# A decoder step on one core: the first part of the time mixing, with its row mixing on ScalarE and one convolution piece to a pair

## The chip, the core and the metric

The kernel runs on one core of a Trainium2 chip, and all of it is one launch. Its engines each work through their own queue in order: TensorE (PE in the profile; its weight loads are PEld), VectorE (DVE), ScalarE (ACT), GpSimd (POOL), and SyncE (SP), which issues most of the DMAs. The metric is the device time of one execution in microseconds (us); lower is better.

## The reference, cut to what matters

One layer of a decoder is computed for 256 prompt rows and 8 samples of 4 rows, 288 rows in all, with a model width of 2048. The part that the change touches is this (`p` holds the weights; the prompt and each sample have their own previous row):

```
p_rkv, p_conv = proj[..., :3 * G_RWKV], proj[..., 3 * G_RWKV:]
p_rkv_prev = jnp.concatenate([(h_last @ w_in[:, :3 * G_RWKV])[:, None], p_rkv[:, :-1]], axis=1)
rkv = p_rkv + (p_rkv_prev - p_rkv) * p['mu_rkv'][l].reshape(-1)
...
kk = (k * p['k_k'][l]).reshape(B, T, N_HEADS, HEAD_SIZE)
kk = kk / jnp.maximum(jnp.sqrt(jnp.sum(kk * kk, axis=-1, keepdims=True)), 1e-12)
k = k * (1 + (a - 1) * p['k_a'][l])
y, S = wkv7_scan(st_wkv[l].astype(f32), r_h, w_h, k_h, v_h, kk, kk * a_h)
...
bg, cg, hc = jnp.split(p_conv, 3, axis=-1)
zc, conv_buf = causal_dwconv(st_conv[l], cg * hc, p['conv_w'][l])
o_conv = bg * zc
```

After it come the output projection and a gated feed-forward block, which the change leaves alone.

## The kernel before

The program has five stages: the conditioning vectors and the first norm; the projection to r, k and v with the first low-rank products; the first part of the time mixing; its second part; the output projection with the feed-forward block. The change lies in the third.

All activations stand transposed, 128 features by 288 rows. The table `A` holds r, k and v as 24 tiles (3 kinds by 8 pairs of heads). Matrix products in float32 are done as three products of a high and a low part: `split` makes the two parts of 1024 weight columns with a cast on ScalarE (L154) and a subtraction on VectorE (L156), and `mm3` issues the three matmuls (L164 to L166).

The third stage starts with `lora2`: 48 matmuls, and 16 sigmoids on ScalarE (L590). Then a loop runs over the 8 pairs. For each pair `lerp` mixes r, k and v with the rows one step earlier (`before`, L341 and L342, and L576); `first` normalises k, scans the decay and scales the operands (a chain over ScalarE, VectorE, TensorE and at its end GpSimd, L597 to L625); `blocks_of` multiplies the pair's 64-row blocks on TensorE and writes them to DRAM. Between these stand `step(cv)` and `step(rest)`. The first emits one piece of the convolution's projection: one weight tile of 1 MB, two splits, 48 matmuls of 288 columns; there are 24 pieces, and after every second one `conv_evac` takes the result out of PSUM. The second emits one step of a conditioning vector (a 1 MB load and 4 matmuls of 512 columns).

After the loop `substitute` reads the blocks back and inverts them by substitution: a sequence of small products and additions on VectorE and GpSimd (L664, L665, 3 steps and then 31), a copy (L666), and three DMAs to DRAM. `drain(cv)` emits the pieces that are left. The second part of the time mixing (`second`, L774 on) begins with loads of the inverse from DRAM (L994 to L998).

The order in the queues of the engines is fixed when the kernel is built: a list scheduler of the framework takes the instructions by their place in the program and by when it thinks they are ready. The scratch tiles of the stage lie by hand in one buffer, `ws`; a ring hands them out in turn, and a tile is written again only when its readers are done.

Of the kernel before, what the change touches and what calls it, by code (L numbers as in the profile page):

```python
# [10 lines left out]
F32 = mybir.dt.float32  # L11
F32R = mybir.dt.float32r
AF = mybir.ActivationFunctionType
# [3 lines left out]
P = 128  # L17
# [6 lines left out]
NP = G // P  # L24
T0 = 256
NB = 8
TS = 4
NT = T0 + NB * TS
NL = T0 + NB * (TS + 1)
LW = NL + 2  # L30
# [49 lines left out]
def kernel(ctx, tc, i, o):  # L80
# [101 lines left out]
    shO = cst.tile([P, 9, KT], F32, name="shO")  # L182
    coO = cst.tile([P, 18, NP], F32, name="coO")
    omka = cst.tile([P, NP], F32, name="omka")

    actx = ctx.enter_context(ExitStack())
    Ap = actx.enter_context(pool("Ap"))
# [52 lines left out]
    cwv = vec[:, 272:296]  # L240
# [74 lines left out]
    def step(g):  # L315
        if g is rest:
            done[0] += 1
        next(g, None)
# [20 lines left out]
    def before(d, a, eng=V):  # L339

        eng.tensor_tensor(d, a[:, 1:1 + NT], a[:, 2:2 + NT], SUB)  # L341
        eng.tensor_tensor(s4(d[:, T0:])[:, :, 0], a[:, 2 + NT:LW], s4(a[:, 2 + T0:2 + NT])[:, :, 0], SUB)  # L342

    def s4(ap):
        return ap.rearrange("p (b t) -> p b t", t=4)
# [9 lines left out]
    with actx:  # L355
# [3 lines left out]
        with pool("x1") as xp:  # L359
# [83 lines left out]
            for bi, (k0, nk) in enumerate(blocks):  # L443
                hs = hn
                last = bi == len(blocks) - 1
                width, part = 2048 // nk, 1024 // nk
                npc = 3 * G // width
                for nb in range(npc):
                    raw = load_piece(w_in, k0, nk, nb * width, width)
                    for ct in range(width // P):  # L450
                        cw = ct * P % part
                        if cw == 0:
                            hv, lv = split(raw[:, :, ct * P:ct * P + part], nk)
                        cw = slice(cw, cw + P)
                        acc = accbank()
                        for kk in range(nk):
                            mm3(acc[:, :NL], hv[:, kk, cw], lv[:, kk, cw],
                                actH[:, k0 + kk], actL[:, k0 + kk], kk == 0, kk == nk - 1)
                        t = nb * width // P + ct
                        if bi == 0:  # L460
                            S.copy(A[:, t, 2:LW], acc[:, :NL])
                        else:
                            V.tensor_tensor(A[:, t, 2:LW], acc[:, :NL], A[:, t, 2:LW], ADD)  # L463
                    if bi == 0 and nb == 0:
                        nc.sync.dma_start(con[:, first:], i['consts'][:, first:NCONST - 2 * P])
                        raw = rawtile()[:, :2 * P]
                        nc.sync.dma_start(raw, i['consts'][:, NCONST - 2 * P:])
                        S.copy(conr, raw.rearrange("p (n x) -> p n x", x=P))
                        turn_rows(2, 4)
                        V.tensor_scalar(omka, kav, -1.0, 1.0, MUL, ADD)  # L470
                        setup.close()
                    for _ in range(0 if last else plan[bi][nb]):
                        step(ada)
                        count += 1
                        if count == 2 * (k0 + nk - blocks[0][1] + blocks[bi + 1][1]):
                            hn = make_h(*blocks[bi + 1])
                    if last and nb == 2:
                        with tc.issue_after(cur['ld'].ins):
                            nc.sync.dma_start(dX, xT)
                    if nb == 0:  # L480
                        raw = rawtile()
                        rw = raw[:, :nk * 448].rearrange("p (k n) -> p k n", k=nk)
                        for name, a, w in (('decay_lora1', 0, 96), ('iclr_lora1', 96, 96), ('gate_lora1', 192, 256)):
                            nc.sync.dma_start(rw[:, :, a:a + w], i[name][0][k0 * P:(k0 + nk) * P]
                                              .rearrange("(k p) n -> p k n", p=P))
                        lps = [bank() for _ in range(4)]
                        for kk in range(nk):
                            if kk % 2 == 0:
                                lwv = split(rw[:, kk:kk + min(2, nk)], min(2, nk))
                            lora1_k(k0 + kk, kk, nk, hs[kk], lwv, lps)  # L490
                        for cidx in range(4):
                            w = 96 if cidx < 2 else 128
                            if bi == 0:
                                S.copy(L1[:w, cidx], lps[cidx][:w, :NT])
                            else:
                                V.tensor_tensor(L1[:w, cidx], lps[cidx][:w, :NT], L1[:w, cidx], ADD)
# [42 lines left out]
        def views(off, *shapes):  # L539
            out = []  # L540
            for shape in shapes:
                ap, off = view(off, shape)
                out.append(ap)
            return out, off

        def ring(off, shape, n):
            aps, off = views(off, *[shape] * n)
            count = [0]

            def turn():  # L550
                count[0] += 1
                return aps[count[0] % n]
            return turn, off

        if True:
            ldr, off = ring(0, (NT,), 2)
            er, off = ring(off, (NT,), 8)
            ntr, off = ring(off, (4, CL), 2)
            nsr, off = ring(off, (NB, TS), 2)
            nrr, off = ring(off, (TS,), 2)  # L560
            cgr, off = ring(off, (2, NT), 1)
            zr, off = ring(off, (NC,), 2)
            zbr, off = ring(off, (NC,), 1)
            (ocv, UL, ULs, TL, TTL, TTs), off = views(off, (NP, NT), (32, 32), (TS, TS), (32, 32), (32, 32), (TS, TS))
            st, off = ring(off, (256,), 1)
            stg, off = ring(off, (256,), 1)

# [3 lines left out]
            def lerp(n, p):  # L571

                t = n * NP + p
                d = ldr()
                before(d, A[:, t])
                V.scalar_tensor_tensor(A[:, t, 2:2 + NT], d, murkv[:, t:t + 1], A[:, t, 2:2 + NT], MUL, ADD)  # L576

            def lora2():
                raw = rawtile().rearrange("p (n x) -> p n x", n=2)
# [12 lines left out]
            def first(p):  # L592
# [23 lines left out]
                V.scalar_tensor_tensor(kk, k, kkv[:, p:p + 1], rn, MUL, MUL)  # L616
                V.scalar_tensor_tensor(XA[:, p], kk, -1.0, cx, MUL, MUL)
                V.tensor_tensor(kk, kk, a, MUL)
                V.tensor_scalar(a, a, kav[:, p:p + 1], omka[:, p:p + 1], MUL, ADD)
                V.tensor_tensor(k, k, a, MUL)  # L620
                GP.tensor_tensor(XB[:, p], kk, ipv, MUL)
                GP.tensor_tensor(k, k, ipv, MUL)
# [71 lines left out]
            def conv_evac(part, j, acc, cg, z):  # L694
                if part == 0:
                    S.copy(cg, acc[:, :NT])
                elif part == 1:
# [5 lines left out]
                    V.tensor_tensor(s6(zb[:, 258:NC])[:, :, 2:6], s4(acc[:, T0:NT]), s4(cg[:, T0:]), MUL)  # L703
                    GP.tensor_copy(coO[:, 0:2, j], zb[:, 256:258])
                    GP.tensor_copy(coO[:, 2:18, j].rearrange("p (b t) -> p b t", t=2), s6(zb[:, 258:NC])[:, :, 4:6])
                    V.tensor_scalar(z[:, :NC - 2], zb[:, 0:NC - 2], cwv[:, j:j + 1], None, MUL)
                    for t in (1, 2):
                        V.scalar_tensor_tensor(z[:, :NC - 2], zb[:, t:NC - 2 + t], cwv[:, 8 * t + j:8 * t + j + 1],
                                               z[:, :NC - 2], MUL, ADD)
# [7 lines left out]
            for p in range(NP):  # L717
                for n in range(3):
                    lerp(n, p)
                first(p)  # L720
                if p:
                    blocks_of(p - 1)
                step(cv)
                step(cv)
                for _ in range(2):
                    step(rest)
# [553 lines left out]
```

## Time and profile before

| | us |
|---|---|
| median of 3 runs | 1698.98 |
| the runs | 1698.98, 1683.72, 1699.15 |
| the profiled execution | 1694.01 |
| its span | 1692.2 |
| PE busy | 1630.8 (96%) |
| DVE busy | 1160.7 (69%) |
| ACT busy | 713.6 (42%) |
| POOL busy | 387.1 (23%) |

The span is that of the profiled execution's instructions, and the busy times are sums over it. The shares are means over five stages, and so they don't say what bounds one of them; the stage of the change runs from about 268 to 491 us of the span. Matmuls overlap, so a stretch in which PE is fully busy can still run at either of two clocks; the granted clock (PEclk, 1.00 is full speed) tells them apart.

### The profile page before, as it was taken

To read this page: it belongs to the slowest core of one execution; us is meant where nothing else is said; L and a number is where in the kernel's file an instruction comes from. 1 tells how busy PE (TensorE), PEld (TensorE's weight loads), DVE (VectorE), ACT (ScalarE), POOL (GpSimd) and SP (SyncE) were. 2 spreads that over 40 slices of the span, in tenths; PEclk is the share of its full clock that TensorE was granted. 3 is DMA by queue.
4 is the path that set the end of the run, shared out by engine and by line. 5 is a ranking of instruction groups with operands and counts; after the bars stand their busy time and mean duration, and the time that the engine had idled before them with its cause. 6 is when DMAs were issued, how large, how long until landed. Compare 5 with 4: busy or idle time off the path is not lost.

```text
span 1692.2 us, 32395 instructions
## 1 busy us (share of the span) xinstructions
PE 1630.8 (96%) x12713; PEld 1481.5 (88%) x12713; DVE 1160.7 (69%) x2464; ACT 713.6 (42%) x1281; POOL 387.1 (23%) x853
## 2 busy tenths in 40 slices
PE   6999999999889999899899999999999999999996
PEld 3778898889866666699799999999999999999996
DVE  3687798977846665554776676757676766757586
ACT  4543355444234433333654343443434343434444
POOL 2132011221633232100143031221213131221212
PEclk9999999999979999999999999999999999999998
DMA  8897865688567667954654545545545445445532
GB/s 274 287 334 270 281 214 191 198 254 258 160 181 248 215 232 247 331 175 141 224 175 150 175 157 168 174 152 173 163 162 174 151 150 183 166 156 169 174 125 76
DMA packets 238306, 333.61 MB, mean 197 GB/s; under 512 B 35698, under 2 KB 180826, under 8 KB 229546
## 3 DMA queue, kind: packets, MB, share of 16 engines
q1 hardware_dynamic: 234937, 324.55, 58.8%
q0 software_dynamic: 2848, 6.20, 1.1%
q8 instruction: 100, 1.64, 0.4%
q10 hardware_dynamic: 368, 0.79, 0.2%
q14 instruction: 53, 0.43, 0.1%
HBM read 321.63 MB, written 9.89 MB: 196 GB/s over the span
## 4 chain that ended last, share of the span: by engine, by line
PE 84%; DVE 8%; ACT 3%; DMA 2%; POOL 1%; issue 1%; SPq 0%; DVEq 0%; ACTq 0%
PE acc L164 22%; PE acc L166 22%; PE acc L165 22%; PE ada L298 5%; DVE wlo L156 2%; PE acc L298 2%; ACT whi L154 1%; PE wb L298 1%; PE wa L298 1%; PE acc L301 1%; PE wa L301 1%; PE ada L301 1%; DMA A<-in_x_sample_dram 1%; PE wb L164 1%; PE wb L166 0%
## 5 line engine op out<-in xcount | busy, mean ns | idle before, releaser
L164 PE MATMUL acc<-actH,whi 128*128 128x288 f32 (+1 forms) x2368 | 707.1, 299 | 9.0 <-ACT whi L154 5.2
L165 PE MATMUL acc<-actL,whi 128*128 128x288 f32 (+1 forms) x2368 | 703.6, 297 | 0.1
L166 PE MATMUL acc<-actH,wlo 128*128 128x288 f32 (+1 forms) x2368 | 700.9, 297 | 2.8 <-DVE wlo L156 2.7
L156 DVE TENSOR_TENSOR wlo<-raw,whi 128x1024 fp32r<-128x1024 f32 (+1 forms) x391 | 478.6, 1226 | 217.3 <-ACT whi L154 211.0
L154 ACT CAST whi<-raw 128x1024 fp32r<-128x1024 f32 x400 | 417.6, 1048 | 475.9 <-PE acc L165 409.3
L164 PEld LDWEIGHTS acc<-actH,whi 128*128 128x128 f32 x2368 | 448.6, 189 | 20.2 <-ACT whi L154 9.7
L166 PEld LDWEIGHTS acc<-actH,wlo 128*128 128x128 f32 x2368 | 447.8, 190 | 5.6 <-DVE wlo L156 4.6
L165 PEld LDWEIGHTS acc<-actL,whi 128*128 128x128 f32 x2368 | 448.3, 189 | 0.4 <-DVE actL L161 0.3
L164 PE MATMUL acc<-gH,whi 128*128 128x288 f32 x704 | 209.1, 297 | 1.7 <-DVE rd L1051 1.7
L166 PE MATMUL acc<-gH,wlo 128*128 128x288 f32 x704 | 210.4, 299 | 0.0
L165 PE MATMUL acc<-gL,whi 128*128 128x288 f32 x704 | 205.7, 292 | 0.0
L1144 POOL COPY uO<-ub 128x2 f32<-128x2 f32 x88 | 24.6, 280 | 548.6 <-ACT ub L1142 548.6
L164 PEld LDWEIGHTS acc<-gH,whi 128*128 128x128 f32 x704 | 132.3, 188 | 3.8 <-PE acc L166 3.7
L165 PEld LDWEIGHTS acc<-gL,whi 128*128 128x128 f32 x704 | 134.0, 190 | 0.0
L166 PEld LDWEIGHTS acc<-gH,wlo 128*128 128x128 f32 x704 | 132.0, 187 | 0.7
L1049 DVE SCALAR_TENSOR_TENSOR xT<-acc,modT,xT 128x256 f32<-128x256 f32 x192 | 91.7, 477 | 27.6 <-PE acc L166 27.6
L301 PE MATMUL ada<-raw,cT 128*32 128x512 f32 x576 | 109.3, 623 | 0.0
L298 PE MATMUL ada<-raw,cT 128*32 128x512 f32 x192 | 100.0, 623 | 1.0 <-DMA raw<-in_ada_w_dram 0.7
L1149 DVE SCALAR_TENSOR_TENSOR uz<-ub,cw,uz 128x304 f32<-128x304 f32 x176 | 96.5, 548 | 4.3
L1141 POOL COPY ub<-sF 128x16 f32<-128x16 f32 x88 | 71.2, 809 | 103.9 <-ACT sF L1045 103.9
L1147 DVE TENSOR_SCALAR uz<-ub,cw 128x304 f32<-128x304 f32 x88 | 33.1, 376 | 49.5 <-ACT ub L1143 49.5
L463 DVE TENSOR_TENSOR A<-acc,A 128x296 f32<-128x296 f32 x96 | 44.2, 463 | 29.0 <-PE acc L166 28.5
(449 smaller groups left out, 1985.0 us busy)
## 6 DMA issues: line engine op xcount, KB each, us to landing
raw<-in_ada_w_dram SPq DMA_DIRECT2D x88, 1024.0 KB, 5.2
raw<-in_ffn_up_dram SPq DMA_DIRECT2D x88, 1024.0 KB, 5.1
raw<-in_w_in_dram SPq DMA_DIRECT2D x48, 1024.0 KB, 7.4
raw<-in_ffn_down_dram SPq DMA_DIRECT2D x44, 1024.0 KB, 5.2
raw<-in_w_out_dram SPq DMA_DIRECT2D x16, 1024.0 KB, 5.9
raw<-in_ada_w_dram SPq DMA_DIRECT2D x16, 512.0 KB, 8.0
dX<-xT SPq DMA_DIRECT2D x1, 2304.0 KB, 16.0
xT<-dX POOLq DMA_DIRECT2D x4, 576.0 KB, 9.3
```

Source lines behind the costliest of these rows:

```text
L154: S.copy(hi, raw)
L156: (GP if cur['share'] and cur['turns'] % cur['share'] == 0 else V).tensor_tensor(lo, raw, hi.bitcast(F32), SUB)
L164: E.matmul(acc, wh, xh, start=start, stop=False)
L165: E.matmul(acc, wh, xl, start=False, stop=False)
L166: E.matmul(acc, wl, xh, start=False, stop=stop)
L298: ins = calls[0]().ins
L301: c()
L463: V.tensor_tensor(A[:, t, 2:LW], acc[:, :NL], A[:, t, 2:LW], ADD)
L1049: V.scalar_tensor_tensor(xT[:, t, :T0], acc[:, :T0], modT[:, m, t, 0:1], xT[:, t, :T0], MUL, ADD)
L1141: GP.tensor_copy(bv[:, :, 0:2], sF[:, :, j].rearrange("p (b t) -> p b t", t=2))
L1147: V.tensor_scalar(z[:, :NC - 2], b[:, 0:NC - 2], cw[:, 0, j:j + 1], None, MUL)
L1149: V.scalar_tensor_tensor(z[:, :NC - 2], b[:, t:NC - 2 + t], cw[:, t, j:j + 1], z[:, :NC - 2], MUL, ADD)
```

## The change

The row mixing is written in another way. Before, VectorE took the difference of the earlier and the present row and added it, weighted, to the present row (three instructions, all on VectorE). Now ScalarE scales the earlier rows by mu (two instructions, the second for the 8 first rows of the samples) and the present rows by 1 - mu (`omur`, made once), and VectorE adds the two. The step that turns `a` into 1 + (a - 1) k_a and the first tap of the convolution move from VectorE to ScalarE. The rings of `first` and of `lerp` have twice as many tiles; the new ones share room with tiles of `substitute`. The loop emits one convolution piece to a pair and not two, so that 16 of 24 pieces stand behind the loop, and not 8.

```diff
+    omur = cst.tile([P, 24], F32, name="omur")
...
+                        V.tensor_scalar(omur, murkv, -1.0, 1.0, MUL, ADD)
...
-            ldr, off = ring(0, (NT,), 2)
-            er, off = ring(off, (NT,), 8)
+            ld_, off = views(0, *[(NT,)] * 2)
+            e_, off = views(off, *[(NT,)] * 8)
...
-            (ocv, UL, ULs, TL, TTL, TTs), off = views(off, (NP, NT), (32, 32), (TS, TS), (32, 32), (32, 32), (TS, TS))
+            more, _ = views(off + NP * NT, *[(NT,)] * 10)
+            (ocv, UL, TL, TTL, ULs, TTs), off = views(off, (NP, NT), (32, 32), (32, 32), (32, 32), (TS, TS), (TS, TS))
+            ldr, er = turns(ld_ + more[8:]), turns(e_ + more[:8])
...
             def lerp(n, p):
                 t = n * NP + p
-                d = ldr()
-                before(d, A[:, t])
-                V.scalar_tensor_tensor(A[:, t, 2:2 + NT], d, murkv[:, t:t + 1], A[:, t, 2:2 + NT], MUL, ADD)
+                a, d, mu = A[:, t], ldr(), murkv[:, t:t + 1]
+                S.activation(d, a[:, 1:1 + NT], AF.Copy, scale=mu)
+                S.activation(s4(d[:, T0:])[:, :, 0], a[:, 2 + NT:LW], AF.Copy, scale=mu)
+                S.activation(a[:, 2:2 + NT], a[:, 2:2 + NT], AF.Copy, scale=omur[:, t:t + 1])
+                V.tensor_tensor(a[:, 2:2 + NT], a[:, 2:2 + NT], d, ADD)
...
-                V.tensor_scalar(a, a, kav[:, p:p + 1], omka[:, p:p + 1], MUL, ADD)
+                S.activation(a, a, AF.Identity, scale=kav[:, p:p + 1], bias=omka[:, p:p + 1])
...
-                    V.tensor_scalar(z[:, :NC - 2], zb[:, 0:NC - 2], cwv[:, j:j + 1], None, MUL)
+                    S.activation(z[:, :NC - 2], zb[:, 0:NC - 2], AF.Copy, scale=cwv[:, j:j + 1])
...
                 step(cv)
-                step(cv)
                 for _ in range(2):
                     step(rest)
```

The change also moves instructions in the queues. Three places matter. (Line numbers of the changed kernel are up to 10 higher: L154 and L160 stay, L590 is now L600, the table load L726, the three instructions of the row mixing on ScalarE L583 to L585, the last one on VectorE L586, and L664 and L665 are now L674 and L675.)

ScalarE at the start of the stage, before: the casts of the last projection, the two casts of `lora2`, the first cast of the convolution, and then the sigmoids.

```order
L154 CAST whi<-raw 128x1024 x5
L160 CAST whi<-raw 96x1024 x2
L154 CAST whi<-raw 128x1024
L590 ACTIVATE XA<-wb,vec 128x288
L590 ACTIVATE XA<-wa,vec 128x288
```

The same place in the changed kernel:

```order
L154 CAST whi<-raw 128x1024 x5
L160 CAST whi<-raw 96x1024 x2
L583 ACTIVATE ws<-A,vec 128x288 x2
L600 ACTIVATE XA<-wb,vec 128x288
L600 ACTIVATE XA<-wa,vec 128x288
```

And what follows there behind the sixteenth sigmoid, down to the convolution's first two casts:

```order
L726 ACT_TABLE_LOAD
L584 ACTIVATE ws<-A,vec 128x8
L585 ACTIVATE A<-A,omur 128x288
L584 ACTIVATE ws<-A,vec 128x8
L585 ACTIVATE A<-A,omur 128x288
L583 ACTIVATE ws<-A,vec 128x288
L623 ACTIVATE ws<-ws 128x288
L584 ACTIVATE ws<-A,vec 128x8
L585 ACTIVATE A<-A,omur 128x288
L607 ACTIVATE ws<-A,vec 128x288
L624 ACTIVATE ws<-ws 128x288
L625 ACTIVATE ws<-ws 128x288
```

The first cast for the convolution has gone from ahead of the sigmoids to behind all of these.

VectorE where the loop ends and the substitution starts, before: behind the last reduction of the blocks (L640) three more splits stand ahead of the substitution's first product (L664).

```order
L640 TENSOR_REDUCE ws<-ws 32x4
L794 COPY ws<-A 128x288
L801 TENSOR_TENSOR ws<-A,pend 128x32
L156 TENSOR_TENSOR wlo<-raw,whi 128x1024 x2
L711 TENSOR_TENSOR ws<-acc,ws 128x256
L712 TENSOR_TENSOR ws<-acc,ws 128x32
L711 TENSOR_TENSOR ws<-acc,ws 128x256
L712 TENSOR_TENSOR ws<-acc,ws 128x32
L156 TENSOR_TENSOR wlo<-raw,whi 128x1024
L664 TENSOR_TENSOR ws<-ws 128x3
```

The same place in the changed kernel (L650 is the reduction, L265 adds a bias to a conditioning vector that TensorE has transposed):

```order
L650 TENSOR_REDUCE ws<-ws 32x4 x2
L810 TENSOR_TENSOR ws<-A,pend 128x32
L810 TENSOR_TENSOR ws<-XB,pend 128x32
L803 COPY ws<-A 128x288
L265 TENSOR_TENSOR modT<-ada,vec 128x4x9 x4
L674 TENSOR_TENSOR ws<-ws 128x3
L156 TENSOR_TENSOR wlo<-raw,whi 128x1024
L675 TENSOR_TENSOR ws<-ws 128x3
L156 TENSOR_TENSOR wlo<-raw,whi 128x1024
```

No split is left between the last reduction and the first product.

VectorE further on, in the changed kernel, from the first of the 31 larger steps: eight of them stand in one row (L674 with up to 192 columns, each followed by its L675) before the next split.

```order
L674 TENSOR_TENSOR ws<-ws 128x156
L675 TENSOR_TENSOR ws<-ws 128x6x26
L674 TENSOR_TENSOR ws<-ws 128x175
L675 TENSOR_TENSOR ws<-ws 128x7x25
L674 TENSOR_TENSOR ws<-ws 128x192
L675 TENSOR_TENSOR ws<-ws 128x8x24
L156 TENSOR_TENSOR wlo<-raw,whi 128x1024
L674 TENSOR_TENSOR ws<-ws 128x184
```

The kernel before has the same eight in a row; what differs is the number of splits ahead of them. Behind the substitution's last step VectorE has 21 further splits of the convolution in the changed kernel, and none in the kernel before.

## Rows read from the trace of the kernel before

**Rows 1.** Stretches: start:end, us, busy us of five engines (instructions), PEclk, DMA share, GB/s.

```profile
268.00:284.00 16.00, 13.98 (x98) 11.12 (x97) 15.77 (x37) 14.36 (x28) 2.65 (x9) 1.00 0.51 161
311.00:413.00 102.00, 102.00 (x808) 89.08 (x804) 82.39 (x177) 44.10 (x77) 23.47 (x47) 1.00 0.80 256
456.00:460.00 4.00, 0.20 (x2) 0.15 (x1) 3.83 (x13) 0.50 (x1) 2.56 (x8) 0.91 0.21 33
460.00:466.00 6.00, 6.00 (x25) 6.00 (x26) 5.35 (x19) 1.91 (x3) 1.14 (x6) 0.50 0.38 153
484.00:502.00 18.00, 15.22 (x136) 11.47 (x134) 5.26 (x15) 3.97 (x13) 4.14 (x17) 0.50 0.78 212
```

**Rows 2.** Timeline of PE: start, us, instruction, and in brackets idle time with its releaser.

```profile
295.39 0.68 PE L635 MATMUL wb<-XA,XB 64*64 64x64 f32 x8 [1.36 <-POOL XB L621]
...
430.06 0.29 PE L164 MATMUL acc<-actH,whi 128*128 128x288 f32 x1
...
440.00 0.30 PE L164 MATMUL acc<-actH,whi 128*128 128x288 f32 x1
...
459.88 0.58 PE L164 MATMUL acc<-actH,whi 128*128 128x288 f32 x1 [3.80 <-DVE ws L703]
...
487.17 0.60 PE L301 MATMUL acc<-T,ws 32*32 32x32 f32 x8 [2.73 <-DMA T<-dT]
```

**Rows 3.** Groups by line and shape, 311 to 413 us: count | busy, mean ns | idle before.

```profile
L156 DVE TENSOR_TENSOR wlo<-raw,whi 128x1024 fp32r<-128x1024 f32 x24 | 29.6, 1246 | 14.0 <-ACT whi L154 13.9
...
L576 DVE SCALAR_TENSOR_TENSOR A<-ws,vec,A 128x288 f32<-128x288 f32 x9 | 5.6, 625 | 0.1
L621 POOL TENSOR_TENSOR XB<-ws 128x288 f32<-128x288 f32 x6 | 5.3, 882 | 6.0 <-DVE A L620 5.6 <-DVE ws L342 0.4
L619 DVE TENSOR_SCALAR XB<-XB,vec,omka 128x288 f32<-128x288 f32 x6 | 3.8, 632 | 0.0
L341 DVE TENSOR_TENSOR ws<-A 128x288 f32<-128x288 f32 x8 | 3.6, 450 | 0.0
...
L342 DVE TENSOR_TENSOR ws<-A 128x8 f32<-128x8 f32 x9 | 2.6, 290 | 0.0
L597 ACT ACTIVATE ws<-A,vec 128x288 f32<-128x288 f32 x4 | 2.1, 536 | 9.9 <-POOL A L622 9.9
L706 DVE TENSOR_SCALAR ws<-ws,vec 128x304 f32<-128x304 f32 x4 | 1.5, 372 | 0.0
```

**Rows 4.** Timeline of ACT at the start of the stage.

```profile
269.18 1.05 ACT L154 CAST whi<-raw 128x1024 fp32r<-128x1024 f32 x1
...
276.92 0.61 ACT L590 ACTIVATE XB<-wa,vec 128x288 f32<-128x288 f32 x1
277.55 1.28 ACT L716 ACT_TABLE_LOAD   x1
...
280.29 1.03 ACT L154 CAST whi<-raw 128x1024 fp32r<-128x1024 f32 x1
```

**Rows 5.** Timeline of DVE behind the loop.

```profile
433.99 0.35 DVE L664 TENSOR_TENSOR ws<-ws 128x31 f32<-128x31 f32 x1
...
441.12 0.52 DVE L665 TENSOR_TENSOR ws<-ws 128x192 f32<-128x192 f32 x1
...
474.75 0.42 DVE L711 TENSOR_TENSOR ws<-acc,ws 128x256 f32<-128x256 f32 x1
```

**Rows 6.** The chain of waits from 413 us: start, us, engine, tile and line.

```profile
413.56 0.60 PE wb L635 x8
...
474.36 2.06 ACT ws L666
...
490.94 0.62 PE wa L892 x2
...
522.29 0.36 PE wa L892 x2
...
547.33 0.36 PE wa L892 x2
```

More of the change, by code (lines that the diff above doesn't have):

```diff
@@ L547, in ring, with turns @@
             aps, off = views(off, *[shape] * n)
+            return turns(aps), off
+        def turns(aps):
             count = [0]
@@ L551, in turn @@
                 count[0] += 1
-                return aps[count[0] % n]
-            return turn, off
+                return aps[count[0] % len(aps)]
+            return turn
         if True:
-            ldr, off = ring(0, (NT,), 2)
-            er, off = ring(off, (NT,), 8)
+            ld_, off = views(0, *[(NT,)] * 2)
+            e_, off = views(off, *[(NT,)] * 8)
             ntr, off = ring(off, (4, CL), 2)
```

## The prediction

> **What bounds the kernel now.** I read the stretches first, then the timelines of TensorE, ScalarE and VectorE in the stage of the change, then the chain of waits. From 311 to 413 us, six turns of the pair loop, TensorE is busy all the time at the full clock, and its timeline has no idle time there; VectorE is busy 82.4 us of 102 and ScalarE 44.1 [rows 1]. So a turn takes 17.0 us and TensorE sets it. Before that VectorE is the bound: from 268 to 284 us it is busy 15.8 us of 16 [rows 1], and at 295.39 TensorE still waits for the pair's operands [rows 2]. Behind the loop the substitution and the splits share VectorE. Its 31 larger steps begin at 433.99 [rows 5] and end with the copy at 474.36 [rows 6], just as the last pieces of the convolution are taken out of PSUM at 474.75 [rows 5]. On the way TensorE waits 3.80 us at 459.88 for a PSUM bank whose reader stands behind substitution steps [rows 2], and after that gap its clock is 0.50, the lower of its levels (1.2 and 2.4 GHz), for 6 us [rows 1]. Then the second part waits for the inverse to come back from DRAM (2.73 us at 487.17, [rows 2]), and the clock is 0.50 again from 484 to 502 us [rows 1]. The first pair of that part takes 31.4 us (490.94 to 522.29), the second 25.0 (to 547.33) [rows 6].
>
> The edits relieve VectorE in a loop that TensorE bounds. They can win only at the start, in the substitution and at the hand-over; TensorE's own work is the same.
>
> **The prices.** A matmul costs 0.1325 us: 75 of them lie between the two of its rows [rows 2], so a piece (48) costs 6.4 us. A row mixing cost VectorE 0.45 + 0.29 + 0.63 = 1.37 us [rows 3]. Now VectorE keeps one addition, 0.45, and ScalarE gets two activations with a scale from a table, nearest to L597 at 0.54, and a small one. No row prices the small one: at least nothing, at most 0.54; I take 0.3, near VectorE's 0.29 for the same 8 columns. The step with k_a goes from 0.63 on VectorE to 0.54 on ScalarE, the first tap from 0.37 to 0.54 [rows 3].
>
> Per pair, VectorE had 82.4 / 6 = 13.7 us, with 9 of 18 mixings in that stretch (the L576 in [rows 3]; the others ran earlier). It loses two splits (2.5, [rows 3]), 1.5 mixings (2.1), 0.6 for k_a and, by my estimate, 0.8 of the convolution's evacuation, and gains three additions (1.4): 9.1. ScalarE had 44.1 / 6 = 7.4. It loses two casts (2.1, [rows 4]) and half the evacuation copies (0.2), and gains three mixings (4.1), k_a (0.5) and taps (0.2): 9.9. TensorE loses one piece: 17.0 - 6.4 = 10.6. TensorE remains the bound, but ScalarE comes within 0.7 us of it and VectorE within 1.5.
>
> **Term A, the start: +5.** The convolution's first cast went ahead of the sigmoids at 269.18 [rows 4]; now it is queued behind them, the table load and eleven activations. The sigmoids and the load end at 278.8 as before (277.55 + 1.28). The eleven, three of them small, follow each other every 0.1 to 0.45 us, together 3.7: the cast starts at 282.5, its split ends at 284.7 (1.03 + 1.25). Until the first blocks TensorE then has 54 matmuls (7.2), a conditioning step (0.9) and the second pair's group sum (0.7): the blocks start at 293.5 and not at 295.4. But by then the kernel before had done 97 convolution matmuls: 43 fewer are 5.7 us, two conditioning steps more give 1.8 back. 5.7 - 1.8 - 1.9 = 2 us behind. TensorE also stands nearly idle from 277 to 282.5, longer than the gap of 3.80; half clock for 6 us costs 3. Ends 0 and 8: the waiting loop work may fill the gap, or the clock may stay low for longer.
>
> **Term B, the pairs: +6.** At 10.6 us a pair the path from one group sum to that pair's blocks gets tight: in queue order all of a turn's VectorE work but one split lies on it (9.1 - 1.2 = 7.9 us), then the product on GpSimd (0.88, [rows 3]) and about 1 us of hand-overs, 9.8 in all. It is hidden while nothing else stands in that path. In the fourth to fifth pair an evacuation with 2.7 us of VectorE work stands there, and in the last three the chains of pairs 6 and 7 run interleaved, with two group sums ahead of one split: 3 + 3. Ends 0 and 19 (second rival). The DMAs of a pair, 3 MB in 10.6 us, are 290 GB/s against 256 at a DMA share of 0.80 [rows 1]; the loads are issued a turn ahead, so I price them at nothing; without that cover they too fall under the upper end.
>
> **Term C, behind the loop: +8.** Before, from the last blocks (413.56, [rows 6]) to 474.75 it took 61.2 us for 384 matmuls, the blocks and a transpose, 53 of work: 8 lost. Now no split stands between the last blocks and the substitution, and VectorE first waits for a transpose that TensorE does only behind piece 7: TensorE waits 2 us for the next split. The eight larger steps in a row take 7.6 us (433.99 to 441.64, [rows 5]), with the small steps and the split behind them 10; TensorE has 5 us of matmuls left then: 5 lost. The evacuation behind substitution steps recurs twice, 4 and 3, and 2 are lost at bank changes: 16. Then 21 splits' worth of matmuls run undisturbed. 16 - 8 = 8; ends 0 (as before) and 14 (half clock after each gap). SP's queue has one convolution load ahead of the reads of the blocks and fifteen behind; the splits wait for VectorE at that point anyway.
>
> **Term D, the hand-over: -5.** From 474.75 to the first product with the inverse, 490.94, it is 16.2 us. Now the inverse is in DRAM some 70 us earlier, and its loads wait only for SP's queue and for room that the last splits free; then the 2.73 and the copy's 2.06 [rows 2, 6] are gone. Ends -7 and 0. **Term E: -5.** Without that wait the clock can stay up: the first pair's 31.4 against 25.0 gives at most 6.3. Ends -6.3 and +3.
>
> Twice the ring costs nothing in time; its readers are done before the last blocks, so the substitution's reads don't wait for it. `omur` is one instruction of 24 columns.
>
> The sum: 5 + 6 + 8 - 5 - 5 = +9 on the profiled execution's 1694.0: **1703 us**. The median of the runs, 1699.0, lies 5 above that execution, the fastest run 10 below; I leave the sum as it is and allow for it in the range.
>
> **The rivals.** First, **faster**: the substitution, early and under 16 pieces, costs TensorE nothing, because the splits keep ahead of it. For it: before, the same steps cost TensorE no more than 8 us. Against it: the queue order just shown. Then the 8 lost before go too: -8 - 5 - 5 = -18, with A and B at nothing: 1676. Chance 0.17, partly taken.
>
> Second, **slower**: ScalarE becomes the bound of the loop. Place: k_a on ScalarE, queued behind the next pair's mixing and a cast, and the product on VectorE and then on GpSimd that wait for it before the blocks can start. It decides when that path exceeds 10.6 us; with a ScalarE of 9.9 busy and two waits of 1.5 us for VectorE, a pair takes 13: 8 x 2.4 = 19 in place of 6, in all 1716, with half clock after such gaps 1722. For it: 9.9 against 10.6. Against it: the ring lets the mixing run a pair ahead. Chance 0.21. The Trainium skill, "ScalarE: Activation LUTs", Rules for kernel authors, would have additions and multiplications on VectorE and not on ScalarE. The rows agree as to sums: a mixing rises from 1.37 us on one engine to 0.45 + 1.38 on two; by the rule alone, with nothing overlapping, 24 mixings cost 24 x 0.46 = 11 us.
>
> Third, **no change**: what moves lies under TensorE's constant work, and A to E cancel within 5 us: 1694 to 1699. Chance 0.12. My forecast has 0.50.
>
> The range, 1683 to 1723, takes in these cases but the outer ends, and the 5 us between execution and median. 1% is 17 us, about what can be told from no change here; by the cases, faster by more has 0.12, slower by more 0.21.
>
> **What the profile would show.** A: no convolution matmul between 277 and 282 us, low clock behind it. B: turns of 10.6 to 12 us; at 13 or more, with waits for XB, the second rival. C: a gap of some 5 us about 20 us behind the last blocks, then solid matmuls for 65 us. D: under 12 us from the last convolution matmul to the first product with the inverse. E: a first pair of some 26 us. Wrong would be: VectorE fully busy in the loop, or no gap in the substitution.

## The result, and the profile after

| | before | after |
|---|---|---|
| median, us (same chip, by turns) | 1698.42 | 1714.5 |
| the profiled execution | 1694.01 | 1713.98 |
| its span | 1692.2 | 1711.5 |
| granted clock, mean | 0.983 | 0.978 |

The changed kernel is slower: the ratio of the runs is 1.0123, with a 95% interval from 1.0087 to 1.0159. (The ratios here and below leave out the three single runs, of 3106 to 8705 us, that were disturbed.) The forecast was 1703 us, 0.5% above the profiled execution. The measured time lies inside the range, and 11 us above the forecast. By its middle the ratio is in the case "slower by over 1%", which had a chance of 0.21, and not in the likeliest (within 1%); the interval reaches below 1%, so the two are not told apart with certainty.

First the timeline of TensorE, with the same columns as [rows 2]: the first blocks, the stalls, the last blocks, the last matmul of the convolution, and the first products with the inverse of the first three pairs of the second part.

```profile
282.09 0.62 PE L299 MATMUL ada<-raw,cT 128*32 128x512 f32 x1 [3.78 <-DMA raw<-in_ada_w_dram]
296.12 0.27 PE L645 MATMUL wb<-XA,XB 64*64 64x64 f32 x1
...
328.02 0.27 PE L645 MATMUL wa<-XA,XB 64*64 64x64 f32 x1 [2.08 <-POOL XB L631]
354.73 0.61 PE L164 MATMUL acc<-actH,whi 128*128 128x288 f32 x1 [1.42 <-ACT whi L154]
367.75 0.27 PE L645 MATMUL wb<-XA,XB 64*64 64x64 f32 x1
381.50 0.48 PE L164 MATMUL acc<-actH,whi 128*128 128x288 f32 x1 [1.59 <-ACT whi L154]
393.79 0.40 PE L166 MATMUL acc<-actH,wlo 128*128 128x288 f32 x1 [3.04 <-DVE wlo L156]
404.58 0.37 PE L164 MATMUL acc<-actH,whi 128*128 128x288 f32 x1 [2.38 <-DVE ws L713]
421.83 0.37 PE L164 MATMUL acc<-actH,whi 128*128 128x288 f32 x1 [3.04 <-DVE ws L674]
...
499.83 0.29 PE L166 MATMUL acc<-actH,wlo 128*128 128x288 f32 x1
513.20 0.47 PE L901 MATMUL wa<-AX,ws 128*128 128x64 f32 x1
541.22 0.32 PE L901 MATMUL wa<-AX,ws 128*128 128x64 f32 x1
566.25 0.32 PE L901 MATMUL wa<-AX,ws 128*128 128x64 f32 x1
```

Of stalls over a microsecond there is one at the start, there are two in the loop (which had none before) and four behind the loop. In the kernel before, the last blocks start at 413.49, the last matmul of the convolution at 474.82, and the first products with the inverse at 490.88 (within 0.1 us of [rows 6]). The second pair's product comes at 541.22 and not at 522.22: 19.0 us late, nearly the whole difference of the spans (19.3). Behind it both kernels take the same 25.03 us a pair. Of the 19.0 us, 1.5 stand there before the stage of the change: the first sigmoid starts at 272.62 us and not at 271.15, and ScalarE's casts come 1.5 us later already at 210 us. So 17.5 us are lost between the sigmoids and the second part's first pair.

The stretches (columns as in [rows 1]):

```profile
276.00:284.00 8.00, 4.22 (x27) 2.73 (x26) 1.38 (x3) 7.98 (x20) 1.20 (x3) 0.92 0.62 230
284.00:292.00 8.00, 7.73 (x38) 4.97 (x37) 6.86 (x13) 8.00 (x19) 1.19 (x3) 0.66 0.79 258
300.00:364.00 64.00, 60.35 (x442) 49.68 (x441) 58.24 (x129) 49.89 (x117) 24.27 (x42) 0.92 0.72 222
380.00:428.00 48.00, 37.90 (x231) 36.69 (x232) 39.00 (x96) 14.22 (x15) 24.02 (x55) 0.86 0.69 196
428.00:492.00 64.00, 64.00 (x480) 63.50 (x478) 30.44 (x41) 25.45 (x31) 2.83 (x16) 1.00 0.48 154
513.00:522.00 9.00, 9.00 (x92) 6.85 (x89) 4.77 (x12) 1.98 (x5) 1.96 (x7) 0.71 0.62 257
```

In the loop VectorE is now busy 91% of the time, TensorE's clock is 0.92, and the full utilisation of [rows 1] is gone. From 380 to 428 us TensorE issues 231 instructions; in the next 64 us, undisturbed, 480, which is 360 in 48.

The prices, as groups of lines by shape from 300 to 364 us (compare [rows 3]):

```profile
L586 DVE TENSOR_TENSOR A<-A,ws 128x288 f32<-128x288 f32 x17 | 8.5, 503 | 0.1
L585 ACT ACTIVATE A<-A,omur 128x288 f32<-128x288 f32 x16 | 8.4, 522 | 0.0
L583 ACT ACTIVATE ws<-A,vec 128x288 f32<-128x288 f32 x15 | 7.4, 524 | 0.0
L584 ACT ACTIVATE ws<-A,vec 128x8 f32<-128x8 f32 x16 | 4.7, 295 | 0.1
L629 ACT ACTIVATE XB<-XB,omka,vec 128x288 f32<-128x288 f32 x7 | 4.4, 625 | 1.9 <-DVE ws L628 1.9
```

A mixing costs ScalarE 1.34 us (1.38 in the prediction, the small one 0.295 against 0.3) and VectorE 0.50. Two prices were off by more than a tenth: that addition, 0.50 against 0.45, and k_a, 0.63 against 0.54.

### The profile page after: what moved, and what is told of

Read it like the earlier page. It is cut to its first block, busy times and chain, and to the rows that moved or that the text cites. A ratio compares the mean times of both kernels' runs of the same rounds, so it can differ in the third digit from the quotient of the medians.

```text
span 1711.5 us, 32432 instructions
## 1 busy us (share of the span) xinstructions
PE 1640.7 (96%) x12713; PEld 1487.8 (87%) x12713; DVE 1144.1 (67%) x2401; ACT 745.8 (44%) x1369; POOL 362.6 (21%) x853
## 4 chain that ended last, share of the span: by engine, by line
PE 82%; DVE 7%; ACT 3%; DMA 3%; POOL 3%; issue 1%; SPq 0%; DVEq 0%; ACTq 0%; POOLq 0%
PE acc L164 22%; PE acc L166 22%; PE acc L165 22%; PE ada L299 4%; PE acc L299 2%; DVE wlo L156 2%; ACT whi L154 1%; PE wb L299 1%; DMA raw<-in_w_in_dram 1%; PE wa L299 1%; PE acc L302 1%; PE wa L302 1%; POOL ws L675 1%; PE ada L302 1%; POOL ws L674 1%
## 5 line engine op out<-in xcount | busy, mean ns | idle before, releaser
L154 ACT CAST whi<-raw 128x1024 fp32r<-128x1024 f32 x400 | 417.7, 1049 | 495.0 <-PE acc L165 412.7
L164 PEld LDWEIGHTS acc<-actH,whi 128*128 128x128 f32 x2368 | 452.1, 191 | 26.5 <-ACT whi L154 12.1
L166 PEld LDWEIGHTS acc<-gH,wlo 128*128 128x128 f32 x704 | 132.3, 188 | 0.8
L165 PEld LDWEIGHTS acc<-gL,whi 128*128 128x128 f32 x704 | 132.3, 188 | 0.0
L1150 POOL COPY ub<-sF 128x16 f32<-128x16 f32 x88 | 53.4, 607 | 103.5 <-ACT sF L1054 103.5
L1151 ACT COPY ub<-acc 128x256 f32<-128x256 f32 x84 | 31.8, 379 | 75.6 <-PE acc L166 75.6
```

Source lines behind the costliest of these rows:

```text
L154: S.copy(hi, raw)
L164: E.matmul(acc, wh, xh, start=start, stop=False)
L165: E.matmul(acc, wh, xl, start=False, stop=False)
L166: E.matmul(acc, wl, xh, start=False, stop=stop)
L1150: GP.tensor_copy(bv[:, :, 0:2], sF[:, :, j].rearrange("p (b t) -> p b t", t=2))
L1151: S.copy(b[:, 2:258], acc[:, :T0])
```

## The experiments

The profiled executions reach the stage up to 4 us earlier or later than the kernel before (the first sigmoid at 267.0 to 275.1 us; at 279.1 where a piece goes ahead of it), so I compare stretches. They are those of one execution of each kernel; the ratio is of its runs. Each is read from that kernel's PE timeline.

| run | first to last blocks | last blocks to last conv matmul | to first product with inverse | first pair | ratio to before, interval |
|---|---|---|---|---|---|
| before | 118.1 | 61.3 | 16.1 | 31.3 | |
| after | 71.6 | 132.1 | 13.4 | 28.0 | 1.0123 [1.0087, 1.0159] |
| one_piece_only | 86.8 | 117.2 | 13.4 | 27.9 | 1.0130 [1.0085, 1.0174] |
| mix_only | 117.6 | 60.0 | 13.9 | 35.6 | 1.0009 [0.9984, 1.0034] |
| no_vector_steps | 72.9 | 135.0 | 12.8 | 28.1 | 1.0181 [1.0128, 1.0235] |
| piece_before_sigmoids | 73.7 | 132.3 | 13.4 | 28.0 | 1.0136 [1.0095, 1.0178] |
| no_substitution | 72.1 | 120.1 | 13.0 | 35.5 | 1.0090 [1.0058, 1.0123] |
| reads_on_gpsimd_queue | 71.4 | 135.0 | 13.4 | 28.2 | 1.0158 [1.0114, 1.0203] |
| ka_on_vector | 72.2 | 134.7 | 13.4 | 28.0 | 1.0120 [1.0098, 1.0141] |
| first_pair_on_vector | 74.2 | 133.2 | 13.3 | 31.3 | 1.0132 [1.0108, 1.0156] |
| steps_between_pieces | 69.9 | 120.6 | 12.8 | 28.1 | 1.0040 [1.0019, 1.0062] |
| twelve_pieces_behind_ordered | 90.8 | 99.8 | 13.0 | 35.5 | 1.0039 [1.0017, 1.0061] |
| twelve_pieces_behind | 88.1 | 105.7 | 13.2 | 31.4 | 1.0083 [1.0054, 1.0112] |
| all_pieces_in_loop_first_on_vector | 118.5 | 60.0 | 14.0 | 35.5 | 0.9980 [0.9958, 1.0003] |

### Which part costs: one_piece_only and mix_only

The first is the kernel before with one piece to a pair; the second is the changed kernel with two.

```diff
 one_piece_only (against before)      mix_only (against after)
-                step(cv)             +                step(cv)
```

> The kernel before with one edit: one convolution piece to a pair in the loop; the mixing stays on VectorE and the rings stay small. My theory (the pair's path over VectorE sets the loop once TensorE has only 10.6 us to a pair): VectorE needs about 12.4 us a pair with its three mixings, so the last blocks start at about 383 us (changed kernel 367.8), the stretch behind the loop loses the same 20 us as in the changed kernel, and the time is about 1729. Rival (ScalarE, loaded with the mixing, is what lengthened the loop): without that load the last blocks start at about 355 and the time is about 1700.

> The changed kernel with two pieces to a pair again: mixing, k_a and tap on ScalarE and the large rings, but eight pieces behind the loop. My theory (the price lies in moving the pieces behind the loop): the loop is bound by TensorE at 17.0 us a pair, the last blocks start at 415 to 418, 61 us from there to the end of the convolution, time 1694 to 1702, the same as before. Rival (the mixing on ScalarE is itself the price): about 1710.

Moving the pieces alone costs 1.3%, as much as the whole change; mixing on ScalarE alone costs nothing that can be measured. The first came out 14 us below what my theory expected. Its loop was as much longer than the changed kernel's as I had said (86.8 us against 71.6); its last blocks come 5 us earlier than expected because the whole stage began 5.5 us earlier than in the changed kernel's execution. What I had wrong is the stretch behind the loop, which I took to be the same and which is 14.9 us shorter. Its loop has 379 matmuls and two conditioning steps less than before (52.0 us), and 384 matmuls stand more behind it (50.9): the loop loses 86.8 - 66.1 = 20.7 us where the changed kernel loses 8.2 (its terms are worked out below), and the stretch behind 117.2 - 112.2 = 5.0 where that loses 11.8. At the start, read from the first sigmoid, it gains 1.6 (first blocks 0.4 earlier, five matmuls fewer and two conditioning steps more done) where that loses 3.5. So mixing on ScalarE does relieve the loop, by 12.5 us, and gives nearly all of it back at the two ends (5.1 and 6.8). The rival, that ScalarE's new work makes the loop longer, is refuted. The Trainium skill, "ScalarE: Activation LUTs", Rules for kernel authors, which would have additions and products on VectorE, is right about the sum (1.84 us on two engines for 1.37 on one), and the time does not follow it: both engines had room under TensorE.

### The start: piece_before_sigmoids, first_pair_on_vector, all_pieces_in_loop_first_on_vector

```diff
 piece_before_sigmoids
+            step(cv)
             lora2()
...
-                step(cv)
+                if p:
+                    step(cv)
 first_pair_on_vector, in lerp
+                if p == 0:
+                    before(d, a)
+                    V.scalar_tensor_tensor(a[:, 2:2 + NT], d, mu, a[:, 2:2 + NT], MUL, ADD)
+                    return
 all_pieces_in_loop_first_on_vector: the same, and in the loop
                 step(cv)
+                step(cv)
```

> The changed kernel with the first piece emitted ahead of the low-rank products and none in the first turn, so that its casts stand ahead of the sigmoids on ScalarE. My theory (term A): the gap from 277 to 282 us fills with matmuls and the clock stays up, the last blocks start about 5 us earlier (363), time about 1709. Rival (the loop takes the gain back, since the pairs' path is what limits it): 367 and 1713.

> The changed kernel, with the three mixings of the first pair (p == 0) on VectorE as they were before, so that the first convolution cast again stands ahead of the sigmoids on ScalarE. Theory (term A is ScalarE's queue order): the gap of 3.78 us at 282 and the low clock behind it go, the first blocks still start at 295 to 296, but one piece more is done by then; the last blocks come at 363 to 364 and the kernel takes 1709 to 1711. Rival (the start only moves, as in the run with the piece ahead of the sigmoids): a gap of the same length at another place, last blocks at 367 to 369, 1713 to 1717.

> The changed kernel with two pieces in every turn, as before, and with the first pair's mixing on VectorE: the mixing on ScalarE alone, without its cost at the start. If term A is ScalarE's queue order, the gap of 4.25 us at 278 us that the run with the mixing alone had is gone and it takes 1690 to 1694; rival (the start waits for something of the same length anyhow): 1695 to 1699, as the kernel before.

ScalarE's timeline in the changed kernel at the place of [rows 4], and the stall that piece_before_sigmoids has in its stead on PE:

```profile
279.00 1.28 ACT L726 ACT_TABLE_LOAD   x1
280.30 0.31 ACT L584 ACTIVATE ws<-A,vec 128x8 f32<-128x8 f32 x1
...
284.01 1.98 ACT L154 CAST whi<-raw 128x1024 fp32r<-128x1024 f32 x2
```

```profile
290.98 0.85 PE L609 MATMUL wa<-ws,conr 128*128 128x288 f32 x1 [3.76 <-ACT ws L607]
```

A piece ahead fills the stall and the first pair's normalisation (L607), still queued behind the mixings, makes it again: 3.76 us in place of 3.78. With the first pair on VectorE the first blocks come 19.5 us behind the first sigmoid and not 23.5 (with 50 matmuls done and not 54; I had expected a piece more), but at one piece a pair those 4 us are given back (2.6 in the loop, 1.1 behind it), so the rival was right there too. With two pieces a pair the gain stays: over 272 to 288 us, mix_only and then all_pieces_in_loop_first_on_vector,

```profile
272.00:288.00 16.00, 11.75 (x75) 8.27 (x74) 10.07 (x17) 15.92 (x36) 2.31 (x6) 0.89 0.63 216
```

```profile
272.00:288.00 16.00, 15.35 (x112) 13.72 (x111) 12.00 (x21) 15.65 (x33) 2.48 (x6) 1.00 0.63 212
```

and the first blocks come 22.2 us behind the first sigmoid and not 27.5, with one conditioning step (0.9) less done, while the loop behind takes 118.5 us against 117.6. The ratio goes from 1.0009 to 0.9980, but the intervals overlap, so a gain in the whole time is not shown. Term A is ScalarE's queue order; in the stretches its cure is kept only where the loop behind is bound by TensorE.

### The second rival's place: ka_on_vector

```diff
-                S.activation(a, a, AF.Identity, scale=kav[:, p:p + 1], bias=omka[:, p:p + 1])
+                V.tensor_scalar(a, a, kav[:, p:p + 1], omka[:, p:p + 1], MUL, ADD)
```

> The changed kernel with the step with k_a (L629) back on VectorE. If the second rival's place were real (k_a behind mixings and casts in ScalarE's queue holds up the blocks), the turns of 12.9, 12.1 and 15.2 us fall by 2 each or more, the last blocks come at 362 and the kernel takes about 1708. My theory, that VectorE's own work and its evacuations lie on that path: 0.63 us more a turn on VectorE takes back what the shorter queue gives; last blocks at 367 to 369, 1713 to 1716.

72.2 us from first to last blocks, against 71.6, and the same ratio. Taking k_a off ScalarE gains nothing. Whether the shorter queue gains something that VectorE's 0.63 us a turn takes back, this run does not tell: of the three turns that the rival named two fall (12.9 to 9.6 us, 15.2 to 10.5) and one rises (12.1 to 13.9), and the fifth goes from 10.9 to 16.0.

### Behind the loop: no_vector_steps, no_substitution, reads_on_gpsimd_queue

```diff
 no_vector_steps
-                        for eng, lo, hi, turn in ((V, 0, 8, st), (GP, 8, n, stg)):
+                        for eng, lo, hi, turn in ((GP, 8, n, stg),):
 no_substitution
-                    for s in range(n - 1):
+                    for s in range(0):
 reads_on_gpsimd_queue (two places)
-                        nc.sync.dma_start(UL[u:u + 32], dN[:, :, x:x + 32, 32 * q:32 * q + 32]
+                        GP.dma_start(UL[u:u + 32], dN[:, :, x:x + 32, 32 * q:32 * q + 32]
```

> The changed kernel without VectorE's share of the substitution's steps (GpSimd's share stays), so that the inverse is not computed. My theory (VectorE's steps between the splits cost TensorE its waits behind the loop): from the last blocks to the end of the convolution 115 us in place of 132, time about 1697. Rival (the waits there come from the loads of the weights or from the low clock alone): 130 us or more and 1712 to 1715.

> The changed kernel without the steps of the substitution on both engines (the blocks are read, copied and written back as they are; the inverse is then not computed). My theory of term C, that the substitution's steps on VectorE stand ahead of the splits and TensorE waits for these: the stretch from the last blocks to the last convolution matmul, 132 us in the changed kernel, falls to 116 to 120 (112 us of matmuls and about 6 at the half clock), and the kernel takes 1699 to 1703 us. Rival, that the convolution's loads are late because they stand behind the reads of the blocks in SyncE's queue: the stretch stays at 126 or more, with casts that wait for their loads some 10 to 25 us behind the last blocks, and the kernel takes 1708 or more.

> The changed kernel, with the reads of the blocks (L658, L663) issued on GpSimd's queue and no longer on SyncE's, so that no convolution load stands behind them. My theory of term C (VectorE's steps hold the splits up): the casts' waits of 6.45 and 2.15 us for their loads go, but the stretch of 132 us shortens by 2 at most: 1712 to 1715. Rival (the loads behind the reads are the cause of the 4 us more that term C cost than forecast): the stretch falls to 124 to 127, 1706 to 1709. Slower than the changed kernel, if the reads come later through GpSimd's steps: 1718.

In the changed kernel four things stand in queues at the same place. Behind the loop DVE's timeline, then the chain of waits, then ACT's timeline (ACTq is a DMA that ScalarE issues):

```profile
385.94 0.19 DVE L674 TENSOR_TENSOR ws<-ws 128x31 f32<-128x31 f32 x1 [1.36 <-DMA ws<-dN]
...
391.88 0.46 DVE L675 TENSOR_TENSOR ws<-ws 128x192 f32<-128x192 f32 x1
392.26 1.48 DVE L156 TENSOR_TENSOR wlo<-raw,whi 128x1024 fp32r<-128x1024 f32 x1
...
412.10 0.43 DVE L712 TENSOR_TENSOR ws<-acc,ws 128x256 f32<-128x256 f32 x1 [3.10 <-POOL coO L714]
```

```profile
381.09 4.68 DMA ws<-dN
...
411.69 0.25 POOL ws L675
411.94 0.13 POOL coO L714
412.10 0.43 DVE ws L712
```

```profile
384.61 0.34 ACTq L677 DMA_DIRECT2D dTs<-ws  x1
388.85 2.00 ACT L154 CAST whi<-raw 128x1024 fp32r<-128x1024 f32 x2 [6.45 <-DMA raw<-in_w_in_dram]
```

(1) The eight larger steps in a row ahead of the split, as forecast. (2) GpSimd's steps ahead of the small copy L714 of the convolution's evacuation: VectorE waits 3.10 us for that copy, and from 386 to 412 the chain of waits runs over GpSimd's steps, so it is GpSimd's half of the substitution, not VectorE's, that ends last there. (3) The convolution's loads behind the reads of the blocks (L663) on SP's queue: a cast waits 6.45 us. I had set that at nothing. (4) The DMAs and the copy L676 of the inverse, on ScalarE's queue ahead of casts; here the first of them is issued at 384.61, before the load that the cast behind it waits for has landed, so it costs nothing yet. SP's timeline:

```profile
379.12 2.64 SPq L663 DMA_DIRECT2D ws<-dN  x4
381.81 14.24 SPq L170 DMA_DIRECT2D raw<-in_w_in_dram  x5
```

Of TensorE's four waits the first ends with a cast that waited for a load, the second with the split behind (1) (its cast was done some 2 us before it began), the third and fourth with VectorE's evacuation steps and what is queued among them.

That is why single cures fail. Without VectorE's steps, (4) takes over: ScalarE stands 16.51 us at L676, waiting for GpSimd, and then TensorE 12.69 us for the cast behind it. With the reads on GpSimd's queue the loads are there, and the cast waits the same time, 6.53 us, for (4):

```profile
413.53 1.93 ACT L676 COPY ws<-ws 64x1024 f32<-64x1024 f32 x1 [16.51 <-POOL ws L675]
```

```profile
380.13 0.36 ACTq L677 DMA_DIRECT2D dTs<-ws  x1
380.53 2.94 ACT L154 CAST whi<-raw 128x1024 fp32r<-128x1024 f32 x3 [6.53 <-DVE ws L675]
```

So no_vector_steps says nothing of my theory, whose expected 115 us did not come, and reads_on_gpsimd_queue refutes the loads as the cause by themselves. Without any of the steps the stretch falls to 120.1 us, the top of what I expected, although a cast still waits 7.00 us for its load. The time, 1709.9 us, is 7 us above what the theory said and the rival's number; the stretch is the theory's. The 7 us lie in the first pair: 35.5 us and not 28.0.

### The order alone: steps_between_pieces

All of the work, in another order of the queues:

```diff
+                        yield                            # behind each step of the substitution
...
-            substitute()
+            sub = substitute()
+            for _ in range(2):
+                step(cv)
+            for _ in range(16):
+                step(cv)
+                with tc.issue_after(cur['sp'].ins):      # the piece's last split
+                    for _ in range(3):
+                        step(sub)
+            drain(sub)
             drain(cv)
```

> The changed kernel with all of its work, in another queue order behind the loop: two convolution pieces are written ahead of the reads of the blocks, and of the substitution's steps three stand behind each following piece's splits instead of in a row. My theory of term C (splits, loads and evacuations stand in queues behind the substitution's steps and reads, several at the same place): the stretch from the last blocks to the last convolution matmul falls from 132 us to 117 to 121, and the time to 1699 to 1706, the upper end if the first pair of the second part runs at the half clock throughout (35 us in place of 28), as it did in the run without the substitution. Rival (the substitution costs by its sums of work on VectorE, whatever its order): the stretch stays at 128 or more, 1711 to 1716.

120.6 us in place of 132.1, and 1701.45 us: the ratio falls from 1.0123 to 1.0040, as expected, two thirds of the loss. The stretch of 48 us after it, beside the row of the changed kernel above (231 instructions at 0.86):

```profile
380.00:428.00 48.00, 45.63 (x328) 44.98 (x329) 34.27 (x59) 18.18 (x20) 25.31 (x46) 0.96 0.77 217
```

That the substitution costs by its sums whatever its order is refuted.

### A version that beats both? twelve_pieces_behind_ordered and twelve_pieces_behind

Both have the first pair on VectorE, and twelve pieces behind the loop. The first also has four steps behind each following piece and one piece ahead of the reads, by the code above.

```diff
                 step(cv)
+                if p < 4:
+                    step(cv)
```

> The changed kernel's mixing on ScalarE (the first pair on VectorE), but two pieces in each of the first four turns and one in the last four, so that twelve stay behind the loop, one of them ahead of the reads, and four of the substitution's steps behind each following piece's splits. By my theory the turns lose 3 to 6 us in place of 13 (the four with two pieces are bound by TensorE), the stretch behind the loop 6 to 8 us over its matmuls, the hand-over and the first pair win 3 each as in the changed kernel: 1689 to 1696, against 1698 of the kernel before 2 to 9 faster. Rival, that each piece moved costs the same 2.5 us (20 us for eight, 10 for four): 1704 to 1709.

> As the run with twelve pieces behind the loop, but with the reads and the substitution's steps written in a row, as in the changed kernel. By my theory the queue order behind the loop alone makes the difference: 8 to 12 us more in the stretch behind the loop than with the steps between the pieces, 1698 to 1706. Rival (order does not matter): the same time as that run within 3 us.

The order is worth 5.9 us in the stretch and 7.3 in the median here (1701.9 against 1709.2), somewhat less than expected. Neither beats the kernel before; 1701.9 us is 6 above the upper end of what I expected, and 2 under the rival's lower. The loop lies where I said: it loses 90.8 - (118.1 - 31.3 - 1.8) = 5.8 us, with 236 matmuls and two conditioning steps fewer. The stretch behind it does not: it loses 99.8 - (61.3 + 31.8 + 1.8) = 4.9 us against the kernel before, which by the prediction's count lost 8 there already, so it is 13 us over its matmuls and not 6 to 8. And the first pair ran 35.5 us in the profiled execution (at 1707.45 us the slowest of its runs) and ate what the hand-over won. Of all versions only those with all pieces in the loop are not slower: 1.0009, and with the first pair on VectorE 0.9980, an interval that just reaches 1. No version beats both kernels by more than can be measured.

## Why the prediction was right or wrong

By its own steps, where each term is a stretch of the table less the work moved: 386 convolution matmuls and four conditioning steps fewer between the first and the last blocks (51.1 and 3.6 us by the prediction's prices), 432 and two more behind (57.2 and 1.8), 46 fewer and two steps more ahead. The first row is no term of the prediction: it is what the profiled execution had lost before the stage.

| term | forecast | measured | how |
|---|---|---|---|
| ahead of the stage | | +1.5 | 272.62 - 271.15, first sigmoids |
| A, start | +5 | +3.5 | first blocks 0.7 later, 6.1 - 1.8 less done, without the 1.5 |
| B, pairs | +6 | +8.2 | 71.6 - (118.1 - 51.1 - 3.6) |
| C, behind the loop | +8 | +11.8 | 132.1 - (61.3 + 57.2 + 1.8) |
| D, hand-over | -5 | -2.7 | 13.4 - 16.1 |
| E, first pair | -5 | -3.3 | 28.0 - 31.3 |
| sum | +9 | +19.0 | 541.22 - 522.22 |

**A was right** in mechanism, and 1.5 us smaller than forecast. (Of matmuls it counted 97 and 54 ahead of the first blocks; the traces have 100 and 54.) TensorE stood until 282.09 (then a load for a conditioning step came; the convolution's first matmul starts at 285.09), and the clock was 0.66 behind. The first cast came at 284.0, 1.5 us later than forecast, as the stage itself began 1.5 us later.

**B was right in kind, and too small.** The turns are 9.7, 9.3, 12.9, 12.1, 10.9 and 15.2 us between the starts of the blocks, then 1.6; the long one is where two chains are interleaved, as forecast. But TensorE does not "remain the bound" with VectorE 1.5 us behind: VectorE is busy 58.2 us of 64, which at 11.7 us a turn is 10.6 and not 9.1. The second rival's turn of 12.9 with a wait for XB is there once (2.08 us at 328.02), but taking its place, k_a, off ScalarE gained nothing (ka_on_vector).

**C is the term that was mis-sized most.** The mechanism, steps ahead of splits, was right: taken away or put in another order, the stretch loses 11.5 to 12 us. The step that failed is the list of queues. I counted VectorE's eight steps and set SP's queue at nothing ("the splits wait for VectorE at that point anyway"), and I did not look at what stands behind GpSimd's steps. Instead of one gap of 5 us some 20 us behind the last blocks there are four, 1.6 to 3.0 us, at 14, 26, 37 and 54 us, and the clock over that stretch is 0.86. How the 11.8 us divide among the queues is not shown, since each single removal uncovers the next wait. Solid matmuls follow from 428 to 500 us, as forecast.

**D was half right.** The inverse is early (the copy L676 begins at 427.06, before at 474.36 [rows 6]), and the wait of 2.73 us is gone. The other 2.3 us of the forecast did not come: 12.8 to 14.0 us of this stretch is there in every version but the kernel before.

**E was half right.** The first pair gained 3.3 of the 6.3 us that were to be had, since the clock falls in the hand-over without any wait for the inverse (0.71 over 513 to 522). That it gained 3.3 is in part luck: this pair takes 28, 31 or 35.5 us in these kernels (last section), and nothing in the prediction tells which.

The misses of B to E have the same sign. Each alone is 2 to 4 us, small beside its own bounds; together they are 10 us. What A came out under its forecast and the 1.5 us ahead of the stage cancel. The first rival (the substitution under 16 pieces costs nothing) falls with C. The second gave 1716 us, next to what was measured, and yet it is not what happened: the step with k_a could go back to VectorE without a change.

## What to carry to other kernels

Where work that filled a tight loop is moved behind it, list for every engine, SP and GpSimd included, what stands in its queue at that place: four waits lay on top of each other here, and taking one away gave nothing (reads_on_gpsimd_queue) or less (no_vector_steps), while putting the work in another order gave back 11.5 us. The loop that TensorE filled had no stalls and no half clock; freeing the other engines inside it was worth nothing that could be measured (mix_only), and taking work out of it uncovered the chain that it hid.

## What the runs showed of the hardware

A step of GpSimd and a split of VectorE hold each other up, each where it is the second to start. In the changed kernel a step that starts during a split takes 1.30 to 1.33 us and not 0.45, and a split that starts during a step takes 1.48 to 1.50 and not 1.22. The split at 392.26 (1.48 us, shown above) starts while the first of these steps runs:

```profile
392.20 0.46 POOL L675 TENSOR_TENSOR ws<-ws 128x128 f32<-128x128 f32 x1
392.74 1.30 POOL L674 TENSOR_TENSOR ws<-ws 128x135 f32<-128x135 f32 x1
```

The one split beside these steps that starts with none running is not longer; there only the step is:

```profile
405.25 1.21 DVE L156 TENSOR_TENSOR wlo<-raw,whi 128x1024 fp32r<-128x1024 f32 x1
405.25 1.50 POOL L675 TENSOR_TENSOR ws<-ws 128x119 f32<-128x119 f32 x1
```

The Trainium skill, "SBUF — State Buffer", Summary: rules for kernel authors, says that of two such operations, VectorE's with two inputs in SBUF, the second waits for the first to finish; the rows agree as to which of them becomes longer, though the split gained 0.26 us where 0.40 of the step were left.

The first pair of the second part takes 28, 31 or 35.5 us for the same work, by the time at which the clock comes back. After its first product TensorE has the granted clock 0.50, the lower of its two levels, for some 5 us more in the changed kernel (to 518.1), for 13 in the kernel before (to 503.6) and for 24 in mix_only (to 509.8), and the pair takes 28.0, 31.3 and 35.6. In no_substitution it was

```profile
501.00:524.00 23.00, 23.00 (x161) 15.79 (x163) 10.45 (x30) 5.68 (x19) 3.52 (x14) 0.50 0.50 189
```

and in steps_between_pieces, behind the same hand-over of 13 us,

```profile
499.00:506.00 7.00, 7.00 (x63) 5.78 (x63) 3.24 (x9) 1.80 (x5) 2.02 (x7) 0.59 0.82 338
506.00:527.00 21.00, 20.60 (x215) 11.75 (x215) 12.58 (x37) 8.94 (x29) 5.08 (x13) 1.00 0.72 237
```

What decides between them was not settled; it is worth 7 us, as much as most of the terms above, and each kernel's value is that of its one profiled execution.
